# Storing the split weights of a hybrid decoder's mixer at two different uses

## The chip, the cores and the metric

The kernel runs on one core of a Trainium2 chip. The metric is the device time of one execution in microseconds. Tensors lie in HBM, and work is done out of the core's on-chip memory by TensorE (matmuls, and weight loads that overlap them), VectorE, ScalarE and GpSimd. SyncE issues most DMA transfers: its queue (SP in the profile) takes its entries strictly one after the other, and an entry that waits holds all that are behind it. In the profile the engines are PE, DVE, ACT and POOL.

## The reference, cut to what matters

One layer of a decoder, for a prompt of 2048 rows with 16 meta rows ahead of it, and for 8 sample groups of 4 rows, with the same weights (float32):

```python
def trunk(x, n_lead, st_lru_conv, st_lru_h, st_ssd_conv, st_ssd, st_ffn_conv, p):
    ...
        h = rmsnorm(x, p['norm_mix'][l])
        m, lc, lh, sc, ss = mixer(h, n_lead, st_lru_conv[l], st_lru_h[l], st_ssd_conv[l], st_ssd[l], p, l)
        x = x + m
        h = rmsnorm(x, p['norm_ffn'][l])
        f, fc = conv_ffn(h, st_ffn_conv[l], p['ffn_w_up'][l], p['ffn_conv_w'][l],
                         p['ffn_conv_b'][l], p['ffn_w_down'][l])
        x = x + f

def mixer(h, n_lead, st_lru_conv, st_lru_h, st_ssd_conv, st_ssd, p, l):
    proj = h @ p['w_in'][l]
    ...
    lru_x, lru_gate, z, xbc, dt_raw = (proj[..., :o1], proj[..., o1:o2], proj[..., o2:o3],
                                       proj[..., o3:o4], proj[..., o4:])
    xc, new_lru_conv = causal_dwconv(lru_x, st_lru_conv, p['lru_conv_w'][l], p['lru_conv_b'][l])
    hl, new_lru_h = rg_lru(xc, st_lru_h, p['lru_wa'][l], p['lru_ba'][l], p['lru_wx'][l], ...)
    lru_out = rmsnorm(hl * jax.nn.gelu(lru_gate), p['lru_out_norm'][l])
    xbc_c, new_ssd_conv = causal_dwconv(xbc, st_ssd_conv, p['ssd_conv_w'][l], p['ssd_conv_b'][l])
    ...
    ys, new_ssd = ssd_chunked(xs, dt, A, Bm, Cm, st_ssd)
    ...
    ssd_out = rmsnorm(ys * jax.nn.silu(z), p['ssd_out_norm'][l])
    out = jnp.concatenate([lru_out, ssd_out], axis=-1) @ p['w_out'][l]
```

The change concerns `h @ p['w_in'][l]` alone: a 1024 by 2560 weight, which the kernel holds as 20 tiles of 128x1024 (512 KB each, all 1024 inputs of 128 outputs).

## The kernel before

The kernel has two phases: the mixer, and the feed-forward part. The mixer goes through the rows in six tiles (`PLAN_A`; called tile 0 to tile 5 here): tile 0 has the samples, the meta rows and 256 rows of the prompt, tiles 1 to 4 have 384 rows each, tile 5 has 256. For every tile all 20 weight tiles of `w_in` are needed again, in the order of their keys 12, 13, ..., 19, 0, 1, ..., 11. "Position 0" is the projection with key 12, "position 1" that with key 13, "position 10" that with key 2, "position 11" that with key 3. In tiles 1 to 4 a few small matmuls for `dt` stand ahead of position 0 and between positions 0 and 1 (`dt_main` L566, `dt_turn` L577).

A product in float32 accuracy is made of three matmuls at TensorE's faster format: a number is split into a high part (rounded to that format) and a low part (the rest), and high by high, high by low and low by high are summed. So each weight tile has to be split before use: ScalarE writes the high part (`divide`, L109, `whi` or `xhi`), VectorE the low part (L110, `wlo` or `xlo`). One projection (`group_mm`, L181) is 24 matmuls, in the order weight high by input high, weight high by input low, weight low by input high, for each eighth of the tile; the third one is the first that needs the low part.

Class `Kept` saves splits. At the first use (tile 0) a weight tile is loaded raw (L120, into `wraw`) and split. At the second use (tile 1) it is loaded raw and split again, and both parts are stored to scratch tensors in HBM (`khi`, `klo`; the store of one tile is issued at the next tile's split, L166, or ahead of the next load of parts, L145). From the third use on (tiles 2 to 5) the two parts are loaded (L152), which is twice the bytes of a raw load and needs no split.

What buffers there are: `wraw` two; `whi`/`wlo` three pairs; `xhi`/`xlo` one pair. Loads of parts take their room from the cycle "rwwxw": "r" is both `wraw` buffers at once, "w" a pair of `whi`/`wlo`, "x" the pair `xhi`/`xlo`. The split that precedes a store takes its room from the cycle "wwwx"; a plain split always takes "w".

What sets the order: TensorE's is fixed by the program (`manual_schedule`). After the first few steps of tile 0, that of the other engines and of the queue is chosen when the kernel is compiled, by a scheduler that moves an instruction ahead of others as far as its data and buffers let it. The loop over `prog` hands out loads ahead of their use (up to `KEPT_AHEAD` = 4 tiles, `AHEAD` = 2 for others) and splits (2 ahead). A tile that is loaded as parts needs no split, and is loaded only once all tiles ahead of it have been split (`if split < loaded: break`).

The names that occur below: `xr` is the copy of a projection out of the accumulator (ScalarE, L553), `cv` its convolution (L556 on ScalarE, L558 three times on VectorE), `th` and `xbc` what follows (L648, L654). `R` (L627, GpSimd) is a table for the state-space part. `xo` and `x` are rows of the residual stream.

Of the kernel before, what the change touches and what calls it, by code (L numbers as in the profile page):

```python
# [73 lines left out]
def build(tc, i, o):  # L74
# [5 lines left out]
    with contextlib.ExitStack() as es:  # L80
# [27 lines left out]
        def divide(hi, lo, raw, E=V):  # L108
            A.activation(hi, raw, AF.Copy)  # L109
            E.tensor_tensor(lo, raw, hi.bitcast(F32), op=SUB)  # L110

        class Plain:


            def __init__(self, src, room=lambda: wp.tile([P, 1024], F32, name="wraw", tag="wraw", bufs=2)):
                self.src, self.room = src, room

            def load(self):
                self.raw = self.room()
                ld(self.raw, self.src)  # L120

            def split(self, E=V):
                hi, lo = (wp.tile([P, 1024], F32R, name=nm, tag=nm) for nm in ("whi", "wlo"))
                divide(hi, lo, self.raw, E)
                self.out = hi, lo, self.raw

        kept, late, done = {}, [], []

        class Kept:
# [4 lines left out]

            def __init__(self, key, src):
                self.key, self.plain = key, Plain(src)
                self.ahead = KEPT_AHEAD

            def load(self):
                self.use = self.uses[self.key] = self.uses.get(self.key, -1) + 1  # L140
                if self.use < 2:
                    self.plain.load()
                    return
                while done:
                    ld(*done.pop(0))  # L145
                room = next(self.rooms)
                if room == "r":
                    parts = [wp.tile([P, 1024], F32, name="wraw", tag="wraw", bufs=2).bitcast(F32R) for z in range(2)]
                else:
                    parts = pair(room)  # L150
                for part, src in zip(parts, kept[self.key]):
                    ld(part.bitcast(F32), src)  # L152
                self.out = (*parts, None)

            def split(self, E=V):
                if self.use == 0:
                    self.plain.split(E)
                    self.out = self.plain.out
                    return
                parts = kept[self.key] = [dp.tile([P, 1024], F32, name=f"{nm}_{self.key}", tag=f"{nm}_{self.key}")  # L160
                                          for nm in ("khi", "klo")]
                hi, lo = pair(next(self.spare))
                divide(hi, lo, self.plain.raw, E)
                self.out = hi, lo, self.plain.raw
                for z in done:
                    ld(*z)  # L166
                done[:] = zip(parts, (hi.bitcast(F32), lo.bitcast(F32)))

        def pair(room):
            pool = pa if room == "x" else wp  # L170
            return [pool.tile([P, 1024], F32R, name=room + nm, tag=room + nm) for nm in ("hi", "lo")]
# [86 lines left out]
        class Halves:  # L258
# [8 lines left out]
            def norm(self, q):  # L267
                rows, load = self.tiles[q]
                x = self.x[q] = k.spare_row() if q == 3 else row_tile()
                y = load(x)  # L270
                r = rstd_of(sum_squares(y[:rows], rows, D), rows, D)
                V.scalar_tensor_tensor(x[:rows], y[:rows], r[:rows], gain[:rows], op0=MUL, op1=MUL)
# [71 lines left out]

        flat = [s if hasattr(s, "load") else Plain(s) for fn, srcs in prog for s in srcs]
        loaded, split, used = 0, 0, 0
        early = sum(len(srcs) for _, srcs in prog[:k.begin_b]) + 2
        begin = contextlib.ExitStack()
        order = {mybir.EngineType.DVE, mybir.EngineType.Activation, mybir.EngineType.Pool}
        begin.enter_context(tc.manual_schedule(engines=order))  # L350
        for n, (fn, srcs) in enumerate(prog):
            if n < START:
                fn()
                continue
            if n == START2:
                begin.close()
            bound = len(flat) if n > k.begin_b else early
            b = n > k.begin_c
            while loaded < bound:
                ahead = LOADS_B if b else LOADS_B1 if n > k.begin_b else getattr(flat[loaded], "ahead", AHEAD)  # L360
                if loaded >= used + len(srcs) + (ahead if n >= START2 else AHEAD):
                    break
                if getattr(flat[loaded], "key", None) in kept:

                    if split < loaded:
                        break
                    split += 1
                flat[loaded].load()
                loaded += 1
            while split < min(loaded, used + len(srcs) + (SPLITS_B if b else AHEAD if n >= START2 else 0)):  # L370
                flat[split].split(*(() if split else (G,)))
                split += 1
            ws = [z.out for z in flat[used:used + len(srcs)]]
            used += len(srcs)
            if fn is k.tail:
                end = es.enter_context(tc.manual_schedule(engines=order))
                continue
            fn(*ws)
# [1083 lines left out]
```

## Time and profile before

| | us |
|---|---|
| median of 3 runs | 2523.54 (2523.44 to 2526.31) |
| the profiled execution | 2520.4 |
| its span, first to last instruction | 2518.5 |
| TensorE busy | 2437.9 (97%) |
| VectorE busy | 1856.4 (74%) |
| ScalarE busy | 1140.5 (45%) |
| GpSimd busy | 691.0 (27%) |
| the mixer's tile 1, from its dt matmuls to tile 2's | 157.7 |
| tile 2, likewise | 149.7 |
| tile 3, likewise | 148.5 |

Mean granted clock of TensorE over the span: 0.992. A row of the timeline reads: start and length in us, engine, line, operation, out<-in, shape, count, and in brackets the engine's idle time before it and what ended it. SPq stands for entries of SyncE's queue. A row of a table by windows reads: from:to in us, length, then busy time and number of instructions of PE, PEld, DVE, ACT and POOL, the granted clock, the share of the DMA engines and GB/s. "DMA to landing" gives smallest, median and largest time in us from the issue of a transfer to its landing. A row of waits gives us in total, how many times, and the longest.

### The profile page before, as it was taken

The numbers are of one execution on the slowest core, as the hardware profiler recorded it, in microseconds if no ns is written. First come the engines' busy times: TensorE is split into PE (matmuls) and PEld (weight loads), VectorE is DVE, ScalarE is ACT, GpSimd is POOL, SyncE is SP. The second block draws the span as 40 slices with busy tenths as digits, with TensorE's granted clock in tenths as the row PEclk, the third lists the DMA queues.
The fourth block names the chain that finished last, engine by engine and source line by source line (L and its number), as shares of the span: only waits on it lengthen the run. The fifth ranks groups of instructions, "written<-read, shape, count | busy, mean of one in ns | idle before, by whom it ended". The sixth has DMA issues, their size and how long they took to land.

```text
span 2518.5 us, 42326 instructions
## 1 busy us (share of the span) xinstructions
PE 2437.9 (97%) x15834; PEld 2220.0 (88%) x15834; DVE 1856.4 (74%) x2948; ACT 1140.5 (45%) x1925; POOL 691.0 (27%) x1059
## 2 busy tenths in 40 slices
PE   7899999999999999999998999999999999999998
PEld 6678899898988888989886999998999998999997
DVE  7879867678675767676777877768877767877766
ACT  5545535344352655454445433435433435433333
POOL 5524323133232344555445101102101102100001
PEclk9999999999999999999999999999999999999999
DMA  5358674654747686464556866665866665866663
GB/s 183 123 190 315 203 274 164 219 201 165 262 143 256 212 246 241 169 234 172 186 199 226 328 225 223 224 227 203 312 221 226 225 228 184 305 220 223 226 218 120
DMA packets 171080, 549.32 MB, mean 218 GB/s; under 512 B 25254, under 2 KB 25638, under 8 KB 170876
## 3 DMA queue, kind: packets, MB, share of 16 engines
q1 hardware_dynamic: 166164, 538.09, 60.9%
q10 hardware_dynamic: 4712, 8.53, 0.9%
q8 instruction: 125, 2.05, 0.3%
q14 instruction: 79, 0.65, 0.1%
HBM read 455.21 MB, written 91.34 MB: 217 GB/s over the span
## 4 chain that ended last, share of the span: by engine, by line
PE 66%; DVE 10%; issue 9%; POOL 6%; ACT 5%; DMA 4%; SPq 0%; POOLq 0%; DVEq 0%; ACTq 0%
PE mm L181 27%; PE sg L1185 14%; PE tr L181 9%; PE yy L181 9%; DVE wlo L110 2%; POOL wraw L1027 2%; ACT whi L109 1%; ACT ws L109 1%; POOL wraw L1026 1%; POOL o_fc L1170 1%; POOL x L1028 1%; DMA wk<-ws 1%; DVE cv L558 1%; PE yy L728 1%; PE yy L740 1%
## 5 line engine op out<-in xcount | busy, mean ns | idle before, releaser
L110 DVE TENSOR_TENSOR wlo<-wraw,whi 128x1024 fp32r<-128x1024 f32 x273 | 344.0, 1261 | 134.8 <-ACT whi L109 132.9
L1185 PE MATMUL sg<-whi,ph 128*128 128x512 f32 x1320 | 423.9, 394 | 6.5 <-DVE acc L1189 6.5
L109 ACT ACTIVATE whi<-wraw 128x1024 fp32r<-128x1024 f32 x274 | 288.8, 1056 | 256.9 <-PE sg L1185 90.2
L181 PE MATMUL mm<-hhi,whi 128*128 128x384 f32 (+4 forms) x1048 | 332.8, 318 | 2.2 <-ACT xr L553 1.8
L181 PE MATMUL mm<-hlo,whi 128*128 128x384 f32 (+4 forms) x1048 | 326.6, 312 | 0.9 <-DVE hlo L256 0.9
L181 PE MATMUL mm<-hhi,wlo 128*128 128x384 f32 (+4 forms) x1048 | 326.8, 312 | 0.0
L1174 DVE SCALAR_TENSOR_TENSOR c<-u,fcw,c 128x512 f32<-128x512 f32 (+1 forms) x384 | 298.4, 791 | 23.9 <-ACT c L1172 14.3
L1185 PEld LDWEIGHTS sg<-whi,ph 128*128 128x128 f32 x1320 | 247.9, 188 | 65.9 <-DVE acc L1189 8.5
L1170 POOL COPY o_fc<-u 128x2 f32<-128x2 f32 x192 | 84.9, 442 | 802.9 <-DVE u L1079 691.9
L1185 PE MATMUL sg<-wlo,ph 128*128 128x512 f32 x660 | 258.7, 392 | 0.6 <-DVE wlo L110 0.6
L1172 ACT ACTIVATE c<-u,fcb,fcw 128x512 f32<-128x512 f32 (+1 forms) x192 | 157.8, 823 | 111.3 <-DVE u L1079 108.8
L181 PEld LDWEIGHTS mm<-hhi,whi 128*128 128x128 f32 x1048 | 201.0, 192 | 5.9 <-ACT xr L553 2.1
L181 PEld LDWEIGHTS mm<-hlo,whi 128*128 128x128 f32 x1048 | 200.6, 191 | 2.7 <-DVE hlo L256 1.2
L181 PEld LDWEIGHTS mm<-hhi,wlo 128*128 128x128 f32 x1048 | 200.5, 191 | 0.2 <-DMA wlo<-klo 0.2
L181 PE MATMUL yy<-h,ws 128*128 128x256 f32 x1476 | 195.4, 282 | 0.0
L181 PE MATMUL tr<-h,ws 128*128 128x256 f32 x1440 | 190.7, 282 | 0.1
L181 PE MATMUL mm<-h,ws 128*128 128x256 f32 x1404 | 185.9, 282 | 0.0
L181 PEld LDWEIGHTS yy<-h,ws 128*128 128x128 f32 x1476 | 184.7, 188 | 1.0
L181 PEld LDWEIGHTS tr<-h,ws 128*128 128x128 f32 x1440 | 180.0, 188 | 1.0 <-issue 0.3
L181 PEld LDWEIGHTS mm<-h,ws 128*128 128x128 f32 x1404 | 175.4, 188 | 0.5
L558 DVE SCALAR_TENSOR_TENSOR cv<-xr,packed,cv 128x384 f32<-128x384 f32 (+2 forms) x216 | 146.4, 679 | 36.9 <-ACT cv L556 33.8
L1185 PEld LDWEIGHTS sg<-wlo,ph 128*128 128x128 f32 x660 | 124.0, 188 | 25.9 <-DVE wlo L110 1.7
(323 smaller groups left out, 5364.4 us busy)
## 6 DMA issues: line engine op xcount, KB each, us to landing
ws<-wk SPq DMA_DIRECT2D x288, 512.0 KB, 4.9
wraw<-in_w_up SPq DMA_DIRECT2D x97, 512.0 KB, 4.8
wk<-ws SPq DMA_DIRECT2D x96, 512.0 KB, 6.0
wraw<-in_w_down SPq DMA_DIRECT2D x94, 512.0 KB, 5.0
wraw<-in_w_out SPq DMA_DIRECT2D x48, 512.0 KB, 3.8
wlo<-klo SPq DMA_DIRECT2D x48, 512.0 KB, 4.8
whi<-khi SPq DMA_DIRECT2D x48, 512.0 KB, 4.2
wraw<-in_w_in SPq DMA_DIRECT2D x40, 512.0 KB, 4.5
```

The costliest lines, as they stand in the source:

```text
L109: A.activation(hi, raw, AF.Copy)
L110: E.tensor_tensor(lo, raw, hi.bitcast(F32), op=SUB)
L181: PE.matmul(ps, l, r, start=(k == 0), stop=(k == len(pairs) - 1))
L558: V.scalar_tensor_tensor(cv[:, 3:W], buf[:, t:t + NC], w[:, t:t + 1], cv[:, 3:W], op0=MUL, op1=ADD)
L728: PE.matmul(psy[z:z + 64, h // 2 * T:(h // 2 + 1) * T], Q.xdt[:T, h * 64:(h + 1) * 64], Q.L3[:, h, :], start=True, stop=True)
L740: PE.matmul(psi[:T, gsl(g)], xbc[6 + g][:, off:off + T], E.S[:, gsl(g)], start=True, stop=True)
L1026: G.tensor_tensor(v1, v0, v1, op=ADD)
L1027: G.tensor_tensor(v0, g0, v0, op=SUB)
L1170: G.tensor_copy(o_fc[:, g, NS, :], u[:, W - 2:W])
L1172: A.activation(cv[:, 2:W], u[:, 2:W], AF.Identity, scale=fcw[:, g, 2:3], bias=c["fcb"][:, g:g + 1])
L1174: V.scalar_tensor_tensor(cv[:, 2:W], u[:, z:z + W - 2], fcw[:, g, z:z + 1], cv[:, 2:W], op0=MUL, op1=ADD)
L1185: PE.matmul(ps, l, r, start=first and n == 0, stop=last and n == len(seq) - 1)
```

## The change

Each `Kept` tile gets a number `first`: 1 for even keys, 2 for odd ones. A tile is loaded raw and split up to and including use `first`; its parts are stored at use `first` and loaded from then on. For even keys that is what it was. Odd keys are split without a store in tile 1, split and stored in tile 2, and loaded as parts in tiles 3 to 5. The third edit only says the same test in another way.

```diff
@@ class Kept, __init__ @@
                 self.key, self.plain = key, Plain(src)
+                self.first = 1 + key % 2
                 self.ahead = KEPT_AHEAD
@@ class Kept, load @@
-                if self.use < 2:
+                if self.use <= self.first:
                     self.plain.load()
                     return
@@ class Kept, split @@
-                if self.use == 0:
+                if self.use < self.first:
                     self.plain.split(E)
                     self.out = self.plain.out
                     return
@@ the loop over prog @@
-                if getattr(flat[loaded], "key", None) in kept:
+                if isinstance(flat[loaded], Kept) and flat[loaded].key in kept:
 
                     if split < loaded:
                         break
                     split += 1
```

One line was added, so from `class Kept` on the changed kernel's line numbers are one higher (L152 becomes L153, L166 becomes L167, L145 becomes L146). The instructions of TensorE are the same in the same order, with other buffers for the weights.

The first place is SyncE's queue where tile 2's first weight tiles are loaded. `khi_12` is the stored high part of key 12, and so on; `in_w_in` is a raw weight tile. Before:

```order
L152 DMA wraw_3527<-khi_12_1994 128x1024
L232 DMA x_4586<-in_x_p 128x1024
L884 DMA xo_3558<-in_x_p 128x512
L152 DMA wlo_3532<-klo_13_2001 128x1024
L152 DMA wraw_3528<-klo_12_1995 128x1024
L152 DMA whi_3531<-khi_13_2000 128x1024
L232 DMA x_4713<-in_x_p 128x1024
L152 DMA whi_3581<-khi_14_2082 128x1024
L152 DMA wlo_3582<-klo_14_2083 128x1024
```

And in the change, from the same load on (`wraw_3491` is key 13, `wraw_3565` key 15):

```order
L153 DMA wraw_3487<-khi_12_1994 128x1024
L233 DMA x_4598<-in_x_p 128x1024
L885 DMA xo_3516<-in_x_p 128x512
L153 DMA wraw_3488<-klo_12_1995 128x1024
L233 DMA x_4731<-in_x_p 128x1024
L885 DMA xo_4836<-in_x_p 128x512
L885 DMA xo_4858<-in_x_p 128x512
L885 DMA xo_4874<-in_x_p 128x512
L120 DMA wraw_3491<-in_w_in 128x1024
L120 DMA wraw_3565<-in_w_in 128x1024
L153 DMA whi_3561<-khi_14_2078 128x1024
L146 DMA khi_13_3539<-whi_3541 128x1024
L146 DMA klo_13_3540<-wlo_3542 128x1024
L153 DMA wlo_3562<-klo_14_2079 128x1024
```

Key 13 comes raw into `wraw`, whose two buffers hold the parts of key 12; behind it stand key 15's raw load, key 14's high part, the two stores of key 13, and only then key 14's low part.

The second place is the same queue around keys 2 and 3 of tile 2. Before:

```order
L152 DMA wraw_3971<-khi_2_2525 128x1024
L152 DMA wraw_3972<-klo_2_2526 128x1024
L152 DMA whi_4013<-khi_3_2569 128x1024
L152 DMA wlo_4014<-klo_3_2570 128x1024
L152 DMA whi_4055<-khi_4_2649 128x1024
L152 DMA wlo_4056<-klo_4_2650 128x1024
```

In the change (`wraw_4041` is key 3, `wraw_4123` key 5):

```order
L153 DMA wraw_4037<-khi_2_2505 128x1024
L146 DMA khi_1_3991<-whi_3993 128x1024
L146 DMA klo_1_3992<-wlo_3994 128x1024
L153 DMA wraw_4038<-klo_2_2506 128x1024
L153 DMA whi_4119<-khi_4_2625 128x1024
L153 DMA wlo_4120<-klo_4_2626 128x1024
L120 DMA wraw_4041<-in_w_in 128x1024
L120 DMA wraw_4123<-in_w_in 128x1024
L146 DMA khi_3_4077<-xhi_4079 128x1024
L146 DMA klo_3_4078<-xlo_4080 128x1024
```

Key 3 again comes raw into buffers that hold the parts of the key before it; it is issued behind key 4's parts.

The third place is VectorE in the first projections of tile 2. Before, no split stands there:

```order
L654 SCALAR_TENSOR_TENSOR xbc_3778<-th,cv 128x384
L558 SCALAR_TENSOR_TENSOR cv<-xr,packed,cv 128x384 x3
L654 SCALAR_TENSOR_TENSOR xbc_3824<-th,cv 128x384
L558 SCALAR_TENSOR_TENSOR cv<-xr,packed,cv 128x384 x3
L654 SCALAR_TENSOR_TENSOR xbc_3866<-th,cv 128x384
```

In the change the splits of keys 17 and 19 stand between the convolutions of key 15:

```order
L655 SCALAR_TENSOR_TENSOR xbc_3740<-th,cv 128x384
L559 SCALAR_TENSOR_TENSOR cv<-xr,packed,cv 128x384 x3
L655 SCALAR_TENSOR_TENSOR xbc_3790<-th,cv 128x384
L110 TENSOR_TENSOR wlo<-wraw,whi 128x1024
L559 SCALAR_TENSOR_TENSOR cv<-xr,packed,cv 128x384 x2
L110 TENSOR_TENSOR wlo<-wraw,whi 128x1024
L559 SCALAR_TENSOR_TENSOR cv<-xr,packed,cv 128x384 x2
L655 SCALAR_TENSOR_TENSOR xbc_3834<-th,cv 128x384
```

## The prediction

> **What bounds the kernel now.** First the page's sums and its chain of waits:
>
> ```profile
> span 2518.5 us, 42326 instructions
> PE 2437.9 (97%) x15834; PEld 2220.0 (88%) x15834; DVE 1856.4 (74%) x2948; ACT 1140.5 (45%) x1925; POOL 691.0 (27%) x1059
> PE 66%; DVE 10%; issue 9%; POOL 6%; ACT 5%; DMA 4%; SPq 0%; POOLq 0%; DVEq 0%; ACTq 0%
> ```
>
> TensorE is busy 97% of the span, so whatever makes it wait, or lowers its clock, is added to the end. The change touches only the mixer's tiles 1 and 2, so next the busy times by tile (tiles 1, 2 and 3, each from its dt matmuls to the next ones):
>
> ```profile
> core 0: us, PE busy (x) PEld busy (x) DVE busy (x) ACT busy (x) POOL busy (x), PEclk, DMA share, GB/s
> 181.90:339.60 157.70, 150.47 (x832) 136.22 (x831) 131.56 (x197) 84.01 (x138) 51.63 (x62) 0.98 0.75 261
> 339.60:489.30 149.70, 147.38 (x831) 133.28 (x830) 108.00 (x178) 67.48 (x119) 45.51 (x62) 1.00 0.58 201
> 489.30:637.80 148.50, 147.11 (x832) 133.47 (x831) 108.01 (x178) 67.52 (x119) 45.53 (x62) 1.00 0.59 204
> ```
>
> The three tiles have the same matmuls. Tile 1, with all 20 splits and all 20 pairs of stores, takes 157.7 us; tile 3, with neither, 148.5. So the work that is now to be spread costs 9.2 us where it stands. What TensorE waited for in tile 1 (us in total, times, longest):
>
> ```profile
> PE yy L728 <- DVE L L681: 2.9, 2, 2.5
> PE sg L778 <- DVE cv L558: 2.5, 1, 2.5
> PE mm L181 <- ACT xr L553: 1.8, 1, 1.8
> ```
>
> 7.2 us of waits, none for a weight and none for a transfer: VectorE and ScalarE are late. In the table TensorE idles 7.2 us in tile 1 and 1.4 in tile 3; the other 3.4 of the 9.2 us are matmuls at a lower clock.
>
> **The change, part by part.** Keys 12, 14, 16, 18, 0, 2, ... (even) are treated as before: split at their second use in tile 1, stored, loaded as parts from tile 2 on. Odd keys are split again in tile 2 and stored there. So 10 of 20 pairs of stores leave tile 1; tile 2 loses 10 loads of parts (1 MB each) and gets 10 raw loads (0.5 MB), 10 splits and 10 pairs of stores. Tile 3 and after are the same.
>
> *Term A, the second projection of tile 2.* Key 12's parts have the room "r", which is both `wraw` buffers. Before, key 13 came as parts into `whi`/`wlo`. Now it comes raw into `wraw`, so its load must wait until the projection of key 12 has read its last weight, and load, split and projection follow one another. In the order this load stands as the first of the queue behind that wait, with key 15's and key 14's behind it. From the moment that releases `wraw`:
>
> ```profile
> 346.39 0.34 PE L181 MATMUL mm<-hlo,wraw 128*128 128x384 f32 x1
> 346.56 0.34 PE L181 MATMUL mm<-hhi,wraw 128*128 128x384 f32 x1
> 346.75 0.33 SPq L152 DMA_DIRECT2D wraw<-khi  x1
> DMA to landing us min/median/max: 5.2/5.2/5.2
> 347.59 0.44 PE L181 MATMUL mm<-hhi,whi 128*128 128x384 f32 x1
> 348.04 0.33 PE L181 MATMUL mm<-hhi,wlo 128*128 128x384 f32 x1
> ```
>
> The trace has the same event already: at 346.75 a load into these very buffers (key 17's high part) is let go by key 12's projection and lands 5.2 us later. There it was four projections early; now it is needed at once. The next such load, at position 10 (rows below), landed in 3.4:
>
> ```profile
> DMA to landing us min/median/max: 3.4/3.4/3.4
> L109 ACT ACTIVATE whi<-wraw 128x1024 fp32r<-128x1024 f32 x274 | 288.8, 1056 | 256.9 <-PE sg L1185 90.2
> L110 DVE TENSOR_TENSOR wlo<-wraw,whi 128x1024 fp32r<-128x1024 f32 x273 | 344.0, 1261 | 134.8 <-ACT whi L109 132.9
> ```
>
> I take the middle, 4.3: 346.75 + 4.3 = 351.05, ScalarE 1.06 and VectorE 1.23 (the undisturbed length in tile 1), with 0.2 for the hand-overs: the low part is there at 353.5. The matmul that first needs it ran at 348.04. Wait: **5.5 us** (4.6 to 6.4 with 3.4 and 5.2). Nothing covers it: TensorE's order is fixed and only the six small dt matmuls (L577) stand between the two projections, already counted in 348.04.
>
> A wait also costs clock. The granted clock in the stretches after three waits:
>
> ```profile
> 209.29 0.44 PE L181 MATMUL mm<-hhi,whi 128*128 128x384 f32 x1 [1.79 <-ACT xr L553]
> 209.50:212.90 3.40, 3.40 (x12) 3.40 (x12) 3.15 (x5) 2.28 (x4) 1.18 (x2) 0.54 0.90 245
> 235.10:238.50 3.40, 3.12 (x18) 2.53 (x19) 2.46 (x5) 2.13 (x4) 0.85 (x3) 1.00 1.01 394
> 53.66 0.70 PE L613 MATMUL yy<-dtm,packed 48*128 48x72 f32 x2 [4.01 <-DVE dtm L608]
> 53.40:59.40 6.00, 5.75 (x22) 5.62 (x23) 4.87 (x9) 0.66 (x3) 4.35 (x3) 0.50 0.27 87
> ```
>
> After 1.79 us of idle half the clock for about 3.4 us (1.7 lost), after 2.5 us at 235 none, after 4.01 us half for 6 us (3.0 lost). For 5.5 us of idle I take **2.5** (1.7 to 3.4). A = 8.0.
>
> *Term B, key 3 behind key 2.* The "r" room comes again with key 2 (position 10), and key 3 is raw:
>
> ```profile
> 393.17 0.34 PE L181 MATMUL mm<-hhi,wraw 128*128 128x384 f32 x1
> 393.36 0.32 SPq L152 DMA_DIRECT2D wraw<-khi  x1
> 396.69 0.71 ACT L783 ACTIVATE th<-th,nk 128x384 f32<-128x384 f32 x1
> 398.00 0.34 PE L181 MATMUL mm<-hhi,wlo 128*128 128x384 f32 x1
> ```
>
> 393.36 + 4.3 + 1.06 + 1.23 + 0.2 = 400.15 against 398.00: **2.1 us** (1.2 to 3.0). Here chunk and gate matmuls between the projections cover the rest; ScalarE is through with its gates at 397.4, before the load lands. Clock: 1.7 or nothing, as after 209 and 235; I take **1.2**. B = 3.3.
>
> The Trainium skill, "TensorE: Matmul & The Clock Gate", section "HAM oscillation — how this bites in real kernels", has TensorE slowed only by idle gaps above some 3.4 us. By that rule B would pay no clock and the total would be 1.2 us less. The row at 209.50 (0.54 after a gap of 1.79 us) speaks against it, the row at 235.10 for it.
>
> *Term C, ten splits more in tile 2.* VectorE gets 10 x 1.23 = 12.3 us and ScalarE 10.6; by the table they idle 41.7 and 82 us there. Tile 1 shows what twenty do, 9.2 us with their stores; half of that, 4.6, is the upper end, none the lower. VectorE catches up during A, and after that two splits (keys 17 and 19) come close to GpSimd's work on R, where one was stretched in tile 1:
>
> ```profile
> 201.44 2.85 DVE L110 TENSOR_TENSOR wlo<-wraw,whi 128x1024 fp32r<-128x1024 f32 x1
> 201.31 1.90 POOL L627 TENSOR_TENSOR Rhi<-packed,dh 128x1024 fp32r<-128x1024 f32 x1
> ```
>
> I take **1.5**.
>
> *Term D, tile 1 with half the stores.* Its 20 splits stay. What stores can do is slow the raw loads (to landing in tile 0, then in tile 1) and so ScalarE:
>
> ```profile
> DMA to landing us min/median/max: 3.3/3.4/4.3
> DMA to landing us min/median/max: 4.1/5.6/6.2
>   DMA wraw<-in_w_in: 7.0, 5
> DVE wlo L110 <- ACT whi L109: 7.9, 8, 1.8
> ```
>
> 2.2 us slower to land, 7.0 us of ScalarE idle, 7.9 of VectorE, which is idle 26 us in that tile anyway. Against that: odd keys no longer use the extra room "x", so splits start later behind TensorE's reads. From -4.6 (half the excess) to +2.5 (one more wait as at 235); I take **-1.0**, near nothing, since the waits end on VectorE and ScalarE whose work stays.
>
> *Sum.* 8.0 + 3.3 + 1.5 - 1.0 = 11.8 us on the profiled execution's 2520.4 (span 2518.5 and 1.9 around it), 2532.2. The median of the runs, 2523.5, is 3.1 above that execution, so 2535. The lower ends add up to 6.3 + 1.2 + 0 - 4.6 = 2.9, the upper to 9.8 + 4.7 + 4.6 + 2.5 = 21.6.
>
> **The rivals.**
>
> *The spreading pays (not slower).* Place: tile 1. If its three waits come from slow raw loads after all, half the stores bring landing back to tile 0's 3.4 us, and the 9.2 us of excess go; with A and B near their lower ends (6.3 and 1.2) and C at nothing the sum is -1.7, 2522; it decides once tile 1 gets below 150 us. For it: DMA share 0.75 in tile 1 against 0.59. Against it: no wait of TensorE there ends on a weight.
>
> *Stores in the way of loads (slower still).* SP takes its entries in turn: key 14's low part is loaded only behind the store of key 13's low part, which waits for VectorE's split, so it is issued at 353.5 at the earliest. With 5.2 us it lands at 358.7; key 13's projection, 4.4 us and 2.5 of clock, ends near 360. So it is just covered. If landings reach the 9.1 us that the slowest part load of this stretch took,
>
> ```profile
> DMA to landing us min/median/max: 3.4/3.7/9.1
> ```
>
> TensorE waits 2.6 us more there, and again for key 16 behind key 15's stores: about 5 us, 2540.
>
> *The change doesn't do what it says* (raw loads not held back) I leave out: two buffers cannot hold three tiles.
>
> **How the numbers follow.** The forecast has 0.68, stores in the way 0.17, the spreading that pays 0.15. The time is the forecast's, 2535; range 2526 to 2545 from the sums of the ends (2.9 and 21.6 on 2523.5). About 0.2%, 5 us, can be told from no change. Faster by more needs the first rival with A at its floor: 0.04. Within 0.2%: the rest of that rival, and 0.02 from the forecast's low end: 0.13. Slower: 0.83.
>
> **What would show it.** A: in tile 2 TensorE's second projection waits 5 to 6 us on VectorE's `wlo` or ScalarE's `whi`, behind a raw load issued when key 12's projection ends, and the granted clock is near 0.5 after it. B: about 2 us before key 3's projection. C: new waits on `cv` or `xr` in tile 2 of 0 to 3 us. D: tile 1 between 153 and 160 us. Tile 3 must stay at 148.5, and the feed-forward part as it is. I am wrong if key 13's load is issued before key 12's projection is over, or if tile 1 drops below 150.

## The result and the profile after

The changed kernel takes **2542.72 us** (median of 4 runs, 2541.77 to 2546.69) against 2523.49 of the kernel before beside it (2522.09 to 2526.31): a ratio of **1.0087, 95% interval 1.0073 to 1.0101**. It is slower, as forecast, but by 19 us (these medians) to 22 us (the ratio) instead of 11.8. The profiled execution took 2541.77, its span and engines are:

```profile
span 2539.8 us, 42343 instructions
PE 2448.0 (96%) x15834; PEld 2229.4 (88%) x15834; DVE 1864.5 (73%) x2958; ACT 1149.7 (45%) x1935; POOL 695.4 (27%) x1059
PE 78%; DVE 11%; DMA 3%; ACT 3%; issue 3%; POOL 2%; SPq 0%; POOLq 0%; DVEq 0%; ACTq 0%
```

The busy times by tile (tiles 1, 2 and 3, from dt matmuls to dt matmuls, as shown of before):

```profile
core 0: us, PE busy (x) PEld busy (x) DVE busy (x) ACT busy (x) POOL busy (x), PEclk, DMA share, GB/s
185.00:350.10 165.10, 152.94 (x831) 137.87 (x830) 132.10 (x197) 83.65 (x137) 51.19 (x62) 0.97 0.53 174
350.10:513.00 162.90, 153.26 (x831) 137.18 (x830) 115.64 (x188) 76.79 (x129) 48.24 (x62) 0.97 0.65 229
513.00:661.80 148.80, 147.41 (x832) 133.46 (x830) 108.02 (x178) 67.51 (x119) 46.33 (x62) 1.00 0.59 204
```

The step from 157.7 to 165.1 in **tile 1** is 7.4 us, that from 149.7 to 162.9 in **tile 2** 13.2; tile 3 is the same within 0.3. So 20.6 of the 21.3 us between the two spans lie in the two tiles that the change touches, and more than a third of it in the one that lost work: half its stores are gone, DMA share 0.75 to 0.53. (Tile 1 also began 2.9 us later, 185.0 against 182.1, and from tile 4 on the span was 2.6 us shorter; in tile 0 the orders of TensorE, VectorE, ScalarE and GpSimd are the same, and run 3 below, with these orders too, began tile 1 at 181.1.) What TensorE waited for in tile 1 (us in total, times, longest):

```profile
PE mm L182 <- ACT xr L554: 3.7, 2, 2.4
PE yy L729 <- DVE L L682: 3.4, 2, 3.0
PE yy L755 <- DVE yt L742: 2.8, 1, 2.8
PE sg L779 <- DVE cv L559: 2.3, 1, 2.3
```

12.2 us of waits instead of 7.2, with one that the kernel before did not have at all (`yt`); the other 2.5 us are matmuls at a lower clock. In tile 2, where the kernel before had 2.3 us of them:

```profile
PE mm L182 <- ACT whi L109: 3.7, 1, 3.7
PE mm L182 <- DVE xlo L110: 1.7, 1, 1.7
PE yy L729 <- DVE L L682: 1.5, 3, 0.6
PE mm L182 <- ACT gq L853: 1.0, 2, 0.6
PE mm L182 <- DVE xo L889: 0.9, 1, 0.9
PE mm L182 <- ACT xhi L109: 0.6, 1, 0.6
PE mm L182 <- DVE wlo L110: 0.3, 1, 0.3
```

The first and the last row are step A, `xlo` and `xhi` step B. The raw load of key 13 on SP, its high part on ScalarE, TensorE's first matmuls with it, and key 14's low part on SP:

```profile
357.08 0.80 SPq L120 DMA_DIRECT2D wraw<-in_w_in  x2
360.58 1.06 ACT L109 ACTIVATE whi<-wraw 128x1024 fp32r<-128x1024 f32 x1 [1.78 <-DMA wraw<-in_w_in]
361.69 0.69 PE L182 MATMUL mm<-hhi,whi 128*128 128x384 f32 x1 [3.71 <-ACT whi L109]
362.95 0.69 PE L182 MATMUL mm<-hhi,wlo 128*128 128x384 f32 x1 [0.25 <-DVE wlo L110]
363.29 0.46 SPq L153 DMA_DIRECT2D wlo<-klo  x1
```

And key 3, behind key 2:

```profile
415.74 0.45 PE L182 MATMUL mm<-hhi,xhi 128*128 128x384 f32 x1 [0.59 <-ACT xhi L109]
418.06 0.44 PE L182 MATMUL mm<-hhi,xlo 128*128 128x384 f32 x1 [1.70 <-DVE xlo L110]
```

The granted clock (PEclk, third from the right) behind A, behind B, and behind a wait of 2.44 us in tile 1:

```profile
360.90:367.70 6.80, 5.75 (x17) 5.25 (x18) 4.96 (x16) 2.10 (x3) 1.63 (x1) 0.52 0.95 316
419.00:422.40 3.40, 3.40 (x13) 3.40 (x12) 1.84 (x2) 0.00 (x0) 3.40 (x2) 0.53 0.96 376
227.80:231.20 3.40, 3.32 (x11) 3.32 (x12) 2.11 (x5) 1.30 (x4) 0.38 (x2) 0.54 0.00 0
```

The waits of A and B are where they were forecast. What was not is tile 1.

### The profile page after: what moved, and what is told of

Its sections match the earlier page's. It is cut to its first block, busy times and chain, and to the rows that moved or that the text cites. A ratio compares the mean times of both kernels' runs of the same rounds, so it can differ in the third digit from the quotient of the medians.

```text
span 2539.8 us, 42343 instructions
## 1 busy us (share of the span) xinstructions
PE 2448.0 (96%) x15834; PEld 2229.4 (88%) x15834; DVE 1864.5 (73%) x2958; ACT 1149.7 (45%) x1935; POOL 695.4 (27%) x1059
## 4 chain that ended last, share of the span: by engine, by line
PE 78%; DVE 11%; DMA 3%; ACT 3%; issue 3%; POOL 2%; SPq 0%; POOLq 0%; DVEq 0%; ACTq 0%
PE mm L182 31%; PE sg L1186 17%; PE yy L182 13%; PE tr L182 9%; DVE wlo L110 2%; PE tr L1186 2%; DVE cv L559 1%; ACT whi L109 1%; DMA wraw<-in_w_out 1%; DVE xi L804 1%; DMA x<-x 1%; PE yy L741 1%; PE yy L729 1%; DMA wraw<-in_w_in 1%; PE tr L252 0%
## 5 line engine op out<-in xcount | busy, mean ns | idle before, releaser
L110 DVE TENSOR_TENSOR wlo<-wraw,whi 128x1024 fp32r<-128x1024 f32 x283 | 357.7, 1265 | 139.6 <-ACT whi L109 137.5
L109 ACT ACTIVATE whi<-wraw 128x1024 fp32r<-128x1024 f32 x284 | 299.5, 1056 | 268.5 <-PE sg L1186 91.8
L182 PE MATMUL mm<-hhi,whi 128*128 128x384 f32 (+4 forms) x1080 | 347.6, 322 | 7.8 <-ACT xr L554 3.7
L182 PE MATMUL mm<-hlo,whi 128*128 128x384 f32 (+4 forms) x1080 | 340.8, 316 | 0.9 <-DVE hlo L257 0.9
L182 PE MATMUL mm<-hhi,wlo 128*128 128x384 f32 (+4 forms) x1080 | 340.4, 315 | 0.3 <-DVE wlo L110 0.3
L182 PEld LDWEIGHTS mm<-hhi,whi 128*128 128x128 f32 x1080 | 209.8, 194 | 11.7 <-ACT xr L554 4.4
L182 PEld LDWEIGHTS mm<-hlo,whi 128*128 128x128 f32 x1080 | 209.5, 194 | 2.7 <-DVE hlo L257 1.2
L182 PEld LDWEIGHTS mm<-hhi,wlo 128*128 128x128 f32 x1080 | 209.3, 194 | 0.8 <-DVE wlo L110 0.8
L1173 ACT ACTIVATE c<-u,fcb,fcw 128x512 f32<-128x512 f32 (+1 forms) x192 | 157.7, 823 | 110.9 <-DVE u L1080 108.4
```

Of the source, the lines that this page charges most:

```text
L182: PE.matmul(ps, l, r, start=(k == 0), stop=(k == len(pairs) - 1))
L1173: A.activation(cv[:, 2:W], u[:, 2:W], AF.Identity, scale=fcw[:, g, 2:3], bias=c["fcb"][:, g:g + 1])
```

## The experiments

Every run is compared with runs of the kernel before beside it (medians 2521.35 to 2522.76). Executions of one kernel lie 10 us apart and more (before: 2516.86 to 2526.86 in one set of 15). The length of a tile and the idle time of TensorE in it come from one profiled execution of each kernel. Tiles with nearly the same idle time had different mean clocks (12.3 us at 1.00 in run 1, 12.2 at 0.97 in the change), so the idle time is given beside the length.

**1. The buffers of the odd splits, in the change.** Odd keys in tile 1 take `whi`/`wlo` or `xhi`/`xlo` in the cycle of before, without a store:

```
-  if self.use < self.first: self.plain.split(E); ...
+  hi, lo = pair(next(self.second if self.use == 1 else self.spare))   # second = cycle("wwwx")
+  divide(hi, lo, self.plain.raw, E); no store if self.use < self.first
```

> The change with one thing put back: in tile 1 the odd keys, which are split there without being stored, take their split's buffers from the same cycle as before (three times `whi`/`wlo`, then once `xhi`/`xlo`) instead of always `whi`/`wlo`. Tile 1 then differs from the kernel before by its ten missing pairs of stores alone; tile 2 has the buffers of the changed kernel. Theory 'rooms' (tile 1 got 7.4 us longer because the odd splits share one pair of buffers and so come behind TensorE's reads): tile 1 returns to 155 to 158 us, the whole to about 2535. Rival 'order' (tile 1 got longer because the missing stores made the scheduler put VectorE's and ScalarE's work in another order, or by the stores themselves): tile 1 stays at 162 to 166, the whole at 2540 to 2543.

2538.51 (ratio 1.0058, 1.0040 to 1.0077). Tile 1 was 160.9 us in the profiled execution, the fastest of six (2530.14), with 12.3 us of idle at a clock of 1.00. So part of the time came back, none of the idle: the length lies between the two expectations.

**2. The same buffers, in the kernel before.**

```
-  hi, lo = pair(next(self.spare))
+  hi, lo = pair("w" if self.key % 2 else next(self.spare))
```

> The kernel before (all twenty keys stored in tile 1, parts loaded from tile 2 on), with one thing taken from the change: the odd keys' splits in tile 1 always go to `whi`/`wlo`. Theory 'rooms': tile 1 becomes 163 to 166 us although all stores are there, tile 2 stays at about 150, the whole at 2529 to 2533. Rival 'order' by the missing stores: tile 1 stays at 156 to 159, the whole at 2522 to 2526.

2522.6 (1.0004, 0.9993 to 1.0014): level. Tile 1 had 9.4 us of idle, 161.2 us, but the time as a whole does not show it. The buffers alone, the first theory, do not make the kernel slower. By the traces the order of VectorE's work in tile 1 is another one here too: against the kernel before, some 40 of its 196 instructions stand elsewhere, as in the change and in run 1. So another order alone need not cost; it matters what stands where.

**3. All stores back in tile 1, in the change.** Odd keys are stored in tile 1 too, to a place that nothing reads, from the buffers of before. Every engine then has the order of before in tile 1.

> The change, but in tile 1 the odd keys are stored as before too, to a place that nothing reads (they are stored again in tile 2, as in the change), in the buffers of before. All engines then have the kernel before's order in tile 1, and tile 2 stays the changed one. Theory 'missing stores' (tile 1 gets longer through what the scheduler and the transfers make of ten pairs of stores less): tile 1 returns to 156 to 161 us with 7 to 9.5 us of idle on TensorE, the whole to 2535 to 2537, that is, before plus tile 2's 13. Rival (tile 1's length is drawn from execution to execution, 157 to 166, by the clock): idle of 11 to 13 us in tile 1 also here, the whole at 2540 or above.

2534.39 (1.0046, 1.0031 to 1.0062), and tile 1 is that of before again:

```profile
181.10:339.50 158.40, 150.75 (x831) 136.17 (x830) 131.47 (x197) 83.87 (x137) 51.70 (x62) 0.98 0.73 248
```

7.7 us of idle. Of the 8.3 us between this kernel and the change (10 by the ratios) tile 1 has 6.7 in the profiled executions; the 12 us between it and the kernel before are tile 2's (162.3 against 149.7). Tile 1 really got longer by leaving ten pairs of stores out and taking the buffers that go with it. The two are not separated by time: the intervals of this run and of run 1, which differ by the stores alone, overlap. By idle time the stores matter whatever the buffers: 7.2, 9.4 and 7.7 us with all of them, 11.0 to 13.5 with half (the change and runs 1, 4 and 5). These are single executions, and the gap from 9.4 to 11.0 is little more than the step from 12.2 to 13.5 between two of them with almost one order (the change and run 4).

**4. No part load of tile 2 into `wraw`, in the change.**

```
+  if room == "r" and self.use == 2:
+      room = "x"
```

> The change, with no part load of tile 2 into the two `wraw` buffers: where the cycle gives 'r' in tile 2 the parts go to `xhi`/`xlo`, so the raw loads behind them need not wait for a projection to end. My steps A and B: tile 2's second projection and key 3's no longer wait, tile 2 goes from 163.0 to 150 to 153 us, the whole to about 2531; what is left above 149.7 is step C. Rival (it is the ten further splits and stores that cost, not the buffer): tile 2 stays above 158, the whole above 2538. Tile 1 stays at about 165 by either.

2539.42 (1.0076, 1.0049 to 1.0102): only 3 us came back, as the rival said. The waits on weights were gone from tile 2, and others stood in their place:

```profile
PE yy L757 <- DVE yt L744: 2.8, 2, 2.5
PE sg L781 <- DVE cv L561: 2.5, 1, 2.5
PE yy L731 <- DVE L L684: 2.0, 2, 1.6
PE mm L184 <- ACT xr L556: 0.9, 1, 0.9
```

These are tile 1's waits. A reading that fits: while TensorE waits 6.3 us for keys 13 and 3, VectorE catches up; take these waits away, and the ten further splits show what they cost.

**5. Runs 1 and 4 together.**

> Both edits: the odd keys' splits in tile 1 in the buffers of before, and no part load of tile 2 into `wraw`. If rooms explain tile 1 and the `wraw` buffer explains tile 2: tile 1 155 to 158, tile 2 150 to 153, the whole 2522 to 2527, so spreading the stores is worth nothing by itself. If spreading them does pay once its side effects are gone: below 2520. If 'order' holds for tile 1: 2530 to 2533.

2536.96 (1.0056, 1.0041 to 1.0071), tile 1 162.9 (11.0 idle), tile 2 158.1 (8.1 idle). None of the three expectations held: with both buffers put right, 14 us stay.

**6. `yt` ahead, in the change.** In tiles 1 and 2 this product gets a higher priority; in VectorE's order that moves two instructions of tile 1, the first of them so:

```
+L742 TENSOR_TENSOR yt<-yy,ex 128x512
 L559 SCALAR_TENSOR_TENSOR cv<-xr,packed,cv 128x384
 L787 SCALAR_TENSOR_TENSOR m<-th 128x384
 L559 SCALAR_TENSOR_TENSOR cv<-xr,packed,cv 128x384
-L742 TENSOR_TENSOR yt<-yy,ex 128x512
```

> The change, with `yt` (the product that TensorE's transposes in the chunks wait for) put in tiles 1 and 2 ahead of other ready work of VectorE. In the program's order this moves two instructions of VectorE in tile 1 and nothing else: the first `yt` goes ahead of two `cv` and the `m` that GpSimd's work on R stretches to 2.24 us, the third ahead of a `gt` and a `ylo`. Theory 'order' (tile 1 got longer because the missing stores made the scheduler place `yt` behind `m` and `cv`, where GpSimd's work stretches them): the wait of 2.8 us on `yt` goes, with half a slow stretch of clock where one follows, tile 1 from 165.1 to 160 to 163 us, the whole to about 2539. Rival (the time of tile 1 is set by the splits, wherever `yt` stands): the wait moves to the next chunk, tile 1 stays above 163.5, the whole above 2541.

2542.25 (1.0077, 1.0064 to 1.0090). The rival was right: the wait on `yt` is gone, and the one on `cv` has taken its place (2.3 to 4.8 us):

```profile
PE sg L781 <- DVE cv L560: 4.8, 2, 3.3
PE mm L182 <- ACT xr L555: 3.8, 2, 2.8
PE yy L730 <- DVE L L683: 3.4, 2, 3.0
```

**7 to 9. More put ahead.** `Gm`, `L`, `yt` and the gates' convolutions with the higher priority in tiles 1 and 2: in the change, in the kernel before, and in run 5's kernel.

```
+  k.ahead_of_others = lambda on: tc.high_priority() if on else contextlib.nullcontext()
+  with k.ahead_of_others(si in (1, 2)): ...
```

> The change, with all of VectorE's work in tiles 1 and 2 that TensorE waits for in the chunks and gates put ahead of other ready work: `Gm`, `L`, `yt` and the convolutions `cv` of the gates. If VectorE is late only because splits and gate work stand ahead of these: the waits on `yt`, `L` and `cv` (together 8.5 us in tile 1) fall below 3 us, tile 1 to 155 to 159, the whole to 2532 to 2536. If VectorE or ScalarE have too much work there whatever the order: the waits stay, in other places, and the whole is at 2540 or above. Steps A and B stay as they are (waits of 3.7 and 2.3 us in tile 2).

2535.57 (1.0052, 1.0033 to 1.0070); tile 1 163.4, idle 10.1.

> The kernel before with the same put ahead (`Gm`, `L`, `yt`, the gates' `cv`, in tiles 1 and 2). If order is what costs: tile 1 from 157.7 (another execution with the same stores: 161.2) to 153 to 155, the whole to 2517 to 2520, faster than both kernels. If not: 2521 to 2526.

2518.91 (0.9992, 0.9983 to 1.0001); tile 1 156.3, idle 6.9.

> The change with the odd keys' buffers of before in tile 1, no part load of tile 2 into `wraw`, and the same put ahead. Without it the two edits gave 2537: tile 1 162.9 and tile 2 158.0, with waits on `cv`, `yt` and `L` in both. If order is what costs: both tiles 152 to 156, the whole 2522 to 2527, so the spread stores neither pay nor cost. If the ten further splits are too much for VectorE in tile 2 whatever the order: tile 2 stays above 156, the whole above 2530.

2524.53 (1.0015, 1.0005 to 1.0025); tile 1 159.3, tile 2 154.0. The whole lies where it was expected if order is what costs, tile 1 does not. By the medians the raised priority gains the change 7 us, run 5's kernel 12, and the kernel before 3.5, which its interval does not tell from nothing. But with the same work put ahead tile 1 is still 7 us longer in the change than in the kernel before.

**10 to 12. The other eight convolutions ahead too**, ScalarE's `xr` with them: in the change, in the kernel before, and there in all six tiles.

> As the run with `Gm`, `L`, `yt` and the gates' `cv` put ahead in the changed kernel (2535.6), and the other eight convolutions of tiles 1 and 2 too: ScalarE's `xr`, which frees TensorE's projection, and their `cv`. If ScalarE holds TensorE because a split that waits for its raw load stands ahead of `xr`: the waits on `xr` in tile 1 (4.9 us, 4 times) fall below 2 us, tile 1 from 163.4 to about 160, the whole to 2531 to 2534. If not: 2535 to 2538.

2533.38 (1.0040, 1.0024 to 1.0057); the waits on `xr` stayed at 4.3 us (4.9 in run 7), though the whole fell as expected. The priority did not take the split away from them all: in this run's trace the first wait (1.7 us) still stands right behind a split that ScalarE began late, after 1.8 us of idle for its raw load (215.72), and only the second (2.6 us) behind a `th` that waited for VectorE. So the split is the cause of the one and not of the other.

> The same in the kernel before (which with the smaller set took 2518.9 against 2522.45). If `xr` behind splits costs there too: its wait in tile 1 of 2.1 us goes, 2515 to 2518. If not: 2518 to 2521.

2518.6 (0.9981, 0.9972 to 0.9991), with 1.7 us of wait on `xr` left: no more than run 8.

> The same in all six tiles of the mixer in the kernel before. Tile 0 has 13.2 us of idle on TensorE, tiles 2 to 4 1.4 to 3.1 us. If order is what costs there too: 2510 to 2515. If tile 0's idle has other causes (its first loads): 2515 to 2520, as with tiles 1 and 2 alone.

2526.7 (1.0020, 1.0008 to 1.0031), outside both expectations: tile 0 got 167.3 us with 18.5 of idle (before: 159.2 and 13.2). Priority is no remedy as such.

**13 to 15. What makes VectorE late.** The longer of the two waits on `xr` in the change's tile 1, 2.44 us, followed back. TensorE and ScalarE first:

```profile
227.88 0.54 PE L182 MATMUL mm<-hhi,whi 128*128 128x384 f32 x1 [2.44 <-ACT xr L554]
226.92 0.52 ACT L649 ACTIVATE th<-cv 128x384 f32<-128x384 f32 x1 [4.41 <-DVE cv L559]
227.35 0.47 ACT L554 ACTIVATE xr<-mm 128x384 f32<-128x384 f32 x1
```

`xr` stands behind `th`, which waited 4.41 us for VectorE's convolution. (The shorter wait, 1.30 us at 221.00, has another cause: its `xr` and `th` stand behind a split whose raw load landed late,

```profile
219.10 1.06 ACT L109 ACTIVATE whi<-wraw 128x1024 fp32r<-128x1024 f32 x1 [1.59 <-DMA wraw<-in_w_in]
```

and that load was issued at 214.90, when VectorE was through with the split before.) VectorE and GpSimd in the microseconds of the longer one:

```profile
220.19 2.69 DVE L110 TENSOR_TENSOR wlo<-wraw,whi 128x1024 fp32r<-128x1024 f32 x1 [0.59 <-ACT whi L109]
222.80 2.25 DVE L655 SCALAR_TENSOR_TENSOR xbc<-th,cv 128x384 f32<-128x384 f32 x1
224.98 1.92 DVE L559 SCALAR_TENSOR_TENSOR cv<-xr,packed,cv 128x384 f32<-128x384 f32 x3
219.90 1.90 POOL L628 TENSOR_TENSOR Rhi<-packed,dh 128x1024 fp32r<-128x1024 f32 x1
221.76 2.88 POOL L628 TENSOR_TENSOR Rlo<-packed,dl 128x1024 fp32r<-128x1024 f32 x1
```

A split that takes 1.23 us alone took 2.69, an `xbc` that takes 0.56 took 2.25: each began while GpSimd worked out a half of R and ended 1.1 and 0.4 us after that half did (221.80, 224.64). The wait on `yt` has the same cause; in the change, VectorE's `m` and `cv` ahead of it:

```profile
254.83 2.24 DVE L787 SCALAR_TENSOR_TENSOR m<-th 128x384 f32<-128x384 f32 x1 [0.72 <-POOL th L786]
256.99 2.25 DVE L559 SCALAR_TENSOR_TENSOR cv<-xr,packed,cv 128x384 f32<-128x384 f32 x1
259.16 0.68 DVE L742 TENSOR_TENSOR yt<-yy,ex 128x512 f32<-128x512 f32 x1
254.76 1.90 POOL L628 TENSOR_TENSOR Rhi<-packed,dh 128x1024 fp32r<-128x1024 f32 x1
256.62 2.21 POOL L628 TENSOR_TENSOR Rlo<-packed,dl 128x1024 fp32r<-128x1024 f32 x1
```

and in the kernel before, where `yt` came just ahead of R (247.98 on GpSimd) and only what nobody waits for was held:

```profile
247.25 0.68 DVE L741 TENSOR_TENSOR yt<-yy,ex 128x512 f32<-128x512 f32 x1
248.38 2.25 DVE L786 SCALAR_TENSOR_TENSOR m<-th 128x384 f32<-128x384 f32 x1
```

The Trainium skill, "SBUF — State Buffer", section "Who interferes with whom", says that a VectorE instruction with two inputs in SBUF contends with a GpSimd instruction that reads SBUF, and that the shared pair of ports is an exclusive lock. These rows agree: the held instructions are such ones, and each ends 0.4 to 1.1 us after the GpSimd instruction that it began beside.

So three kernels had R cut down in tiles 1 and 2, with the order of every other engine as it was: the change, the kernel before, and run 5's kernel.

```
+  n = 8 if si in (1, 2) else T          # columns of R per head, of 128
-  G.tensor_tensor(r[:T, 0:8 * T]..., masks(q)[0]..., d[...], op=MUL)
+  G.tensor_tensor(r[:T, 0:8 * T]...[:, :, :n], ...)
```

> The change with part of the computation left out: in tiles 1 and 2 GpSimd works out only 8 of every 128 columns of R (the rest of R is what tile 0 left there, so these tiles' chunks and the outputs that follow are wrong). Every other engine's instructions and their order stay the same. Theory 'stretch' (TensorE's waits in tile 1 come from VectorE's instructions that run beside GpSimd's two products of R and are stretched to 2.2 to 2.9 us; the changed order puts splits, `xbc` and `yt` there): without them the four kinds of wait in tile 1, 12.2 us of idle, fall to 4 to 6, tile 1 to 151 to 155 us, tile 2 to 159 to 162 (steps A and B stay). Rival 'too many splits in a row': idle in tile 1 stays at 10 or more, tile 1 above 160.

2533.83 (1.0045, 1.0030 to 1.0060). Of the four waits in tile 1 those on `xr` and `yt` are all but gone (0.8 us), those on `cv` and `L` are not (3.3, 3.4): idle 8.5 us, between the two expectations, and tile 1, 160.3 us, where the rival had it (in the slowest of six executions, 2539.96).

> The kernel before with the same part left out (R in tiles 1 and 2). Theory 'stretch': idle in tile 1 falls from 7.2 to 3 to 4 us, tile 1 from 157.7 to 150 to 153, and the difference of the changed kernel's tile 1 to this one's shrinks from 7.4 to below 3 us. Rival: idle stays at 6 to 7 and the difference at 7.

2514.96 (0.9969, 0.9959 to 0.9979); idle 3.8 us in tile 1. The difference in length between the two kernels' tile 1 stayed, 7.8 us, against this theory's expectation: the hold had cost the kernel before nearly as much idle time (3.4 us) as the change (3.7), and by the medians 7 us against 9.

> The change with the odd keys' buffers of before in tile 1 and no part load of tile 2 into `wraw` (2537; tile 2 158.0 with 8.1 us of idle and no wait on a weight), with the same part of R left out in tiles 1 and 2. Theory 'stretch': what the ten further splits cost in tile 2 once steps A and B are gone is the same as in tile 1, so idle in tile 2 falls to 2 to 4 us and tile 2 to 149 to 152. Rival: tile 2 stays at 156 or above.

2518.95 (0.9982, 0.9971 to 0.9993). Here it held to the full; of the waits of run 4 in tile 2 only that on `L` is left at its 2.0 us, with 0.3 on `yt` and on `xo`, 2.6 us of idle in all. By the medians R was worth 18 us in this kernel. Tiles 1 and 2 (this execution, 2512.16, is the fastest of ten):

```profile
181.10:334.40 153.30, 148.05 (x831) 133.33 (x830) 123.41 (x198) 85.04 (x138) 43.12 (x62) 1.00 0.61 202
334.40:484.80 150.40, 147.83 (x832) 133.37 (x831) 112.54 (x187) 75.70 (x128) 39.44 (x62) 1.00 0.66 235
```

Read together, by TensorE's idle time in tile 1 (us; one execution each; along a row the order of every other engine's work in the tile is the same, but for run 1):

| | R as it was | R small |
|---|---|---|
| all stores (the kernel before; run 14) | 7.2 | 3.8 |
| half the stores, the change's buffers (the change; run 13) | 12.2 | 8.5 |
| half the stores, the buffers of before (runs 1 and 5; run 15) | 12.3 and 11.0 | 5.2 |

Only without the hold and with the odd splits in the buffers of before does tile 1 with half the stores come near that with all of them (5.2 and 3.8 us of idle, 153.3 and 152.5 us long). So there are **two causes, and either keeps tile 1 idle without the other**: GpSimd's R, in the order that half the stores bring (11 to 12 us with the buffers of before), and the one ring of buffers for the odd splits (8.5 us with the small R). The buffers too come with an order of their own, so the second is the buffers and their order together. What is left in run 13 on VectorE ahead of the gate:

```profile
232.52 1.23 DVE L110 TENSOR_TENSOR wlo<-wraw,whi 128x1024 fp32r<-128x1024 f32 x1 [0.77 <-ACT whi L109]
233.66 1.92 DVE L559 SCALAR_TENSOR_TENSOR cv<-xr,packed,cv 128x384 f32<-128x384 f32 x3
```

VectorE stands idle 0.77 us for a split's high part and then does the split, with the gate's convolution queued behind it; TensorE waits 3.3 us for that convolution.

**16 to 18. R moved instead of cut.** The kernel of run 11 (more put ahead, before) with tile 1's R on VectorE, and on ScalarE; and the change with everything found so far undone, R of tiles 1 and 2 on VectorE.

```
-  G.tensor_tensor(r..., masks(q)[0]..., d[...], op=MUL)
+  (V if si in (1,) else G).tensor_tensor(...)                        # first run
+  for h in range(8): A.activation(r[:T, h*T:(h+1)*T], masks(q)[0], AF.Copy, scale=d[:T, q, h:h+1])   # second
```

> The kernel before with `xr`, `cv`, `Gm`, `L` and `yt` put ahead in tiles 1 and 2 (2518.6), and the products of R in tile 1 worked out by VectorE instead of GpSimd, which leaves nothing out. With nothing on GpSimd to stretch VectorE beside it, VectorE gets six products of about 1.25 us more and loses the 1.6 us by which each of some eight instructions is stretched. Theory 'stretch': tile 1 from 157.3 to 152 to 156 us, the whole to 2514 to 2517. Rival (the added 7.5 us of VectorE's work costs what the stretching did): tile 1 stays at 157 or more, the whole at 2518 to 2522.

2512.77 (0.9967, 0.9954 to 0.9979); tile 1 153.2, idle 4.3: as the theory said, the whole a little below its range.

> The same with R of tile 1 on ScalarE, as 48 scaled copies of 128x128. Theory 'stretch': VectorE gains all that it lost beside GpSimd, tile 1 to 151 to 154 us as with the small R, the whole to 2512 to 2516. Rival (ScalarE's copies, some 12 to 17 us more in its order, hold `xr` and `th`): tile 1 at 157 or above, the whole at 2518 or above.

**2510.96 (0.9963, 0.9950 to 0.9975)**, tile 1 152.4, idle 4.5: both versions beat the kernel before, the second by 10 us. Of tile 1's waits only the gate's `cv` and three short ones (1.2 us and below) are left:

```profile
PE sg L791 <- DVE cv L559: 2.5, 1, 2.5
```

> The change without its side effects as far as found: the odd keys' buffers of before in tile 1, no part load of tile 2 into `wraw`, the same work put ahead, and R of tiles 1 and 2 on VectorE. If all that the spreading costs is named by now: tile 1 153 to 157, tile 2 150 to 153, the whole 2517 to 2523, level with the kernel before. If it pays then: below 2516. If something is missing: above 2525.

2520.55 (0.9993, 0.9983 to 1.0004); tile 1 153.3, tile 2 148.8. The first expectation: the change without its side effects is level with the kernel before. Against that kernel with like help (run 16, where only tile 1's R is moved) its profiled tiles 1 and 2 are 0.1 and 1.1 us longer, its median 8. The profiled execution is its fastest; the others reach from 2516 to 2526, and where they lose that was not seen. By either figure spreading the stores gains nothing by itself.

## Why the prediction was right and wrong

*What bounds the kernel.* Right: TensorE, and whatever makes it wait. Right too that tile 1's waits end on VectorE and ScalarE and not on a weight. I did not ask why these are late while VectorE idles 26 us in that tile, and there the failed step begins.

*A (8.0).* The mechanism was right in every part: key 13's raw load is issued when key 12's projection ends, load, split and projection follow one another. The wait is 3.7 + 0.25 = 4.0 us, below my 4.6, since the load landed in 3.5 us and not in 4.3, and TensorE starts on the high part without waiting for the low one. The clock is a little larger: 0.52 over 6.8 us, in which TensorE was busy for 5.75, so 2.8 lost instead of 2.5. Matmul for matmul TensorE stands 7.0 us further back in the tile behind A than in the kernel before (353.59, 13.8 us into the tile, is now 370.92, 20.8 into it). A measured 7.0.

*B (3.3).* Right: 2.3 us of wait (2.1 forecast), a clock of 0.53 over 3.4 us (1.6 lost; 1.2 was a mean of two cases). Behind key 3 TensorE stands 11.4 us further back (401.47 has become 423.22), so B measured 4.4. Runs 13 and 15 give A and B together in another way: 161.5 - 150.4 = 11.1 us of tile 2 with the small R, against 11.4 from the trace and 11.3 forecast; that it is so close is in part luck, since these are the slowest and the fastest execution of their kernels.

By the rule of the Trainium skill that was weighed ("TensorE: Matmul & The Clock Gate", "HAM oscillation — how this bites in real kernels") B's clock should have cost nothing, its gap being 1.7 us. It did cost (0.53 behind it); so did the 2.4 us gap at 227.88 in tile 1 (0.54). The rows decide.

*C (1.5).* Right as a number, 13.2 - 11.4 = 1.8, and, as far as run 4 shows it, by the cover named there: VectorE catches up during A. What I did not say is the price without that cover. My upper end of 4.6, half of tile 1's excess, is too small: in run 5, with A and B gone, tile 2 stayed 8.4 us above before's. With the small R it is 1.4. So A, B and C do not add up as separate terms, and undoing A and B gives back 3 us and not 11.

***D (-1.0) is the step that failed:* tile 1 took 7.4 us more by the trace; the medians of run 3 and the change lie 8.3 us apart.** It was outside its own range (-4.6 to +2.5), and its sign was wrong. The step took tile 1's work to stay as it was but for faster loads: it looked for the effect of the missing stores on the raw loads, as traffic. That traffic did fall, DMA share 0.75 to 0.53, and the raw loads landed in 4.5 us instead of 5.6 (medians), and yet ScalarE's idle for them rose from 7.0 to 9.4 us, VectorE's for ScalarE's high parts (`wlo` behind `whi`) from 7.9 to 13.4. It named the other effect in half a sentence, that the odd splits no longer use the room "x", but took it for a later start of the splits with at most one more wait. Two things took its place. The scheduler, with ten pairs of buffers no longer held by a store, put VectorE's and ScalarE's work of tile 1 in another order, though the diff moves none of it; that order lets the two halves of R hold instructions that TensorE waits for (`xbc` ahead of `xr`, `m` and `cv` ahead of `yt`; the waits of 2.44 and 2.78 us behind them at 227.88 and 259.99). And the splits crowd on one ring of buffers, ahead of the gates' convolutions. That I quoted the hold myself, 2.85 us for a split beside GpSimd's 1.90, and used it only for C's size, makes it the more instructive: a row of the hold stood in the prediction, under another term. The hold alone does not explain D, though: with R small the change's tile 1 was still 4.7 us more idle than the kernel before's.

How much of D is either cause stays open: by time, the stores alone (run 3 to run 1) are 4 us by the medians and 3 by the ratios, the buffers (run 1 to the change) 4 and 7, both with overlapping intervals, and in the kernel before the buffers are nothing (run 2). That the scheduler's order, and not some effect of the transfers, is what the missing stores act through, rests on the runs with a small R, which keep the order; a kernel with before's order in tile 1 and half the stores was not run.

*The rivals.* Stores in the way of loads on SP: not seen. Key 14's low part was issued at 363.29, behind key 13's stores, 13.2 us into the tile; 13.9 was forecast, and no projection waited for it (in runs 1, 7, 10 and 13, with the same loads, TensorE waited 0.3 to 0.7 us in tile 2 for a low part's landing). Spreading that pays: no, tile 1 is longer with it, and run 18 shows nothing to gain once all is undone.

*What would show it.* A, B and tile 3 came where they were said, A with 4.0 us of wait instead of 5 to 6. C's new waits came on `L` and `gq` and not on `cv` or `xr`. D's mark, tile 1 between 153 and 160, is what showed the error.

## What to carry to other kernels

When a scheduler decides the order, a change of buffers or stores in one tile can change every engine's order in that tile: compare the orders there too, and price the difference, before calling a tile untouched. When an engine is late though it has idle time, look for its stretched instructions first (one duration far above the mean of its form) and for what runs beside them; moving that work was worth 6 to 8 us in the kernel before (runs 16 and 17 against run 11), where raising priorities was worth 4 (run 11; 12 in run 5's kernel, by run 9). And a wait of the bounding engine is free time for the late ones: the price of work that stands beside such a wait has to be given for the day that the wait is gone.

## What the hardware showed beyond that

- VectorE's instructions with two inputs in SBUF stood still beside GpSimd's products of 128x1024: 0.55 us became 2.24, 1.23 became 2.69. Over tile 1 of the kernel before, VectorE's busy time fell from 131.5 to 123.2 us once R was small: some 8 us of its "work" was standing still, and counted as busy.
- Equal idle did not mean equal clock. With 12.3 us of idle in tile 1 run 1 kept a granted clock of 1.00, with 12.2 the change had 0.97, which is all of the 4.2 us between these two tiles (TensorE busy 148.6 and 152.9 us).
- 48 scaled copies of 128x128 on ScalarE (13 us of its time in tile 1) cost TensorE one wait of 0.3 us.
